# Four small tiles of a one-core diffusion step made larger, so that the tiles behind them start elsewhere in the partition

## The chip, the cores and the metric

The kernel runs on one core of one Trainium2 chip. Its time is the device time of one execution in microseconds (us); the profile's page, its trace and three timed runs of the kernel before are at hand.

## The reference, cut to what matters

One layer of a hybrid trunk: a shared input projection feeds a gated position-mixing group (A) and a latent-attention group (B); the two are gated, concatenated and projected out. 1024 latent tokens and 128 context tokens, width 1024, all in float32.

```python
def _front(x, cond, norm_g, w_ada, b_ada, w_in, w_s, b_s, g_v, q_norm_g, w_uq, kv_norm_g):
    mod = jax.nn.silu(cond) @ w_ada + b_ada
    shift, scale, gate = jnp.split(mod[:, None, :], 3, axis=-1)
    h = _rmsnorm(x, norm_g) * (1 + scale) + shift
    u, v, g_a, c_q, c_kv, k_rope, g_b = _split_in(h @ w_in)
    a_out = _chunk_mlp(u, v, w_s, b_s, g_v) * jax.nn.silu(g_a)
    ...
def _block_attention(q_nope, q_ropes, key_sets):
    ...
        s = jnp.concatenate(logits, axis=-1).astype(jnp.float32) * ATTN_SCALE
        p = jax.nn.softmax(s, axis=-1).astype(v_all.dtype)
        return jnp.einsum('bhqk,bkhv->bqhv', p, v_all)
    ...
def _back(x, gate, a_out, attn, g_b, w_o):
    y = jnp.concatenate([a_out, attn * jax.nn.silu(g_b)], axis=-1) @ w_o
    return x + gate * y
```

## The kernel before, in words

Every large product is made of three TensorE passes. An operand is split into a high part of fewer bits and the remainder (`lo_of`, line 112, makes the remainder on VectorE), and high by high, high by low and low by high are summed in PSUM. In this text a product, or pass, is one matmul of 128 rows by so many columns: its stationary operand is a 128x128 block of 512 bytes in each partition, its moving operand has 128 partitions by 256, 384, 448 or 512 columns of 4 bytes.

The stages, in order of time:
- 0 to 60 us: the inputs `x` and the conditioning weights `ada` are loaded (SP's queue), the conditioning is multiplied out, the tokens are normalised and turned, and the first products `vacc` are made (512 columns).
- 60 to 235 us: twelve blocks of 128 channels, as two-by-two block products with sums of blocks (`pair_steps`): `p` (line 928, 504 passes) and `tp` (line 949, 288 passes), all of 384 columns. Their stationary operands are the split weights `w` and the split sums `s`; the moving ones are the split tokens in `area` and their sums in `w1t`.
- 235 to 310 us: the query and key projections, `zacc` (lines 1371 to 1373, 448 columns), `qr` and `qn` (lines 158 to 160, 256 and 384 columns).
- 310 to 515 us: attention. Scores `s` (512 and 256 columns), transposes `pT` of the softmax output `e`, and `o` (lines 1633 to 1635, 256 columns; moving operands `ph` and `pl`).
- 515 to 599 us: the output projection, again as block products (`three`, lines 1970 to 1972, 512 columns): results `S` and `A`. The seven products of each of the four `PAIRS` of token tiles read as moving operand one of seven matrices. Two of these, T1 and T4, are read back from DRAM into tiles of the last pool `ep`: T1 wholly (`t1a`, `t1c`, `t1h`, `t1l`, 12 passes a pair), T4 by half (`t4`, 6 passes a pair; the trace drops the number and prints `t`), the other half lies in `vht` and `vlt` of the pool `kv`. The last products `left` (lines 1999 to 2001) have 256 columns.

Each engine's order is written out by planners (`Plan`, `merged`) with fixed costs. They don't know addresses.

Tiles lie in pools; a pool gives each tile a fixed place, rounded up to 32 bytes in the partition, one behind the other. Pools of the left side grow upwards, those of the right side downwards, each from where its neighbour ends. So a small tile sets where all that is laid out behind it starts. Of the built program, the start of a tile in its partition, as the remainder by 128 bytes:

| tiles | before | after the change |
|---|---|---|
| `area`, `w1t`, the keys and values (`kch` to `vl`, later `vht`, `vlt`), the rings `ringB`, `ringC`, `ml`, `mixA`, `ident` | 0 | 0 |
| pool `va` behind `sel`: `x`, `ada`, `w2r`, `w`, `s`, `rows` | 64 | 0 |
| the rest of `va` behind `selr` (`hf`), and of the pools `vb` and `vg` what takes part in products: `gv`, `wsT`, `adag` | 96 | 0 |
| right side below `warm_e`: `mixB`, `cqh`, `cql`, `wfh`, `wfl`, `z`, `e`, `ph`, `pl`, `os`, `t4`, `t1a`, `t1c`, `t1h`, `t1l`, `xr` | 96 | 0 |
| `wuv` (in the first pool) | 96 | 96 |

By 256 bytes, `x`, `ada` and `w2r` start at a remainder of 192 before and of 0 after.

The four tiles themselves hold a scalar or two: `early` and `warm_e` take the output of an activation that is made only to load a table, `sel` and `selr` are two columns that pick sums.

Of the kernel before, what the change touches and what calls it, by code (L numbers as in the profile page):

```python
# [9 lines left out]
F32 = mybir.dt.float32  # L10
F32R = mybir.dt.float32r
# [7 lines left out]
P = 128  # L19
# [70 lines left out]
def f32(ap):  # L90
    return ap.bitcast(F32)
# [3 lines left out]
def tile_hymba_step(ctx: ExitStack, tc: tile.TileContext, I, O):  # L95
# [3 lines left out]
    def opened(name, bufs=1, space=None, side=None):  # L99
        kw = dict(name=name, bufs=bufs, reuse_waits="tile")  # L100
        if space is not None:
            kw["space"] = space
        if side is not None:
            kw["side"] = side
        cm = tc.tile_pool(**kw)
        return cm, cm.__enter__()

    def closed(cm):
        cm.__exit__(None, None, None)
# [120 lines left out]
    c_sm, sm = opened("sm", bufs=2, side="right")  # L230
# [31 lines left out]
    c_va, va = opened("va", side="left")  # L262
# [5 lines left out]
    csp = va.tile([P, 8, 32], F32, tag="csp", name="csp")  # L268
    V.memset(csp, 0.0)
    cs = csp[:, :, 0:2].rearrange("p k c -> p c k")  # L270
    early = va.tile([P, 1], F32, tag="early", name="early")
    tc.keep_in_program_order(S.activation(early, ones[:, 0:1], AF.Silu))
    tc.keep_in_program_order(S.activation(cs, condT, AF.Silu))
    tc.keep_in_program_order(S.activation(early, ones[:, 0:1], AF.Sqrt))

    sel = va.tile([P, 2], F32, tag="sel", name="sel")
    V.tensor_reduce(sel, ident.rearrange("p (j c) -> p c j", j=4)[:, 0:2, :], axis=AX.X, op=ALU.add)

    def slot(i, name, shape, dt=F32):
# [170 lines left out]
    warm = psa.tile([P, 512], F32, tag="acc", name="warm")  # L450
# [553 lines left out]
        for c, g, m, key, room in ((i, 0, "x", "kx", "tm"), (j, 1, "d", "ke", "kd"), (j, 0, "c", "kf", "kc"), (i, 1, "a", "kh", a_room)):  # L1004
            gated(c, g, lambda m=m: keep[m], [f"{key}{n}"], (room,), lambda m=m: keep[m])

    selr = va.tile([P, 2], F32R, tag="selr", name="selr")
    V.tensor_copy(selr, sel)

    def gate_steps(j):  # L1010
# [149 lines left out]
    def rope_weights():  # L1160
        for q in range(2):
            src = rope_raw[:, q * 256 : (q + 1) * 256]
            S.activation(wrh[:, q, :], src, AF.Copy, scale=qgT[:, q : q + 1])
            V.scalar_tensor_tensor(wrl[:, q, :], src, qgT[:, q : q + 1], f32(wrh[:, q, :]), op0=ALU.mult, op1=ALU.subtract)
# [72 lines left out]
    def cq_transpose(t):  # L1237
        last = t == NT - 1
        ps = (psa if last else pst).tile([P, 512], F32, tag="acc" if last else "t", name=f"cqT{t}")
        for q in range(2):  # L1240
            T.transpose(ps[:, q * P : (q + 1) * P], zt[t][:, q * P : (q + 1) * P], ident)
        src = ps[:, 0:256].rearrange("p (q c) -> p q c", q=2)
        dh = cqh[:, :, t * P : (t + 1) * P]

        def low():
            lo_of(cql[:, :, t * P : (t + 1) * P], src, dh)
            made.add(("cq", t))

        later(0.05 if last else 0.4, lambda: S.copy(dh, src))
        later(0.42 if last else 0.85, low)  # L1250
# [6 lines left out]
    def q_nope(g, h):  # L1257
        need(*[("cq", t) for t in range(3 * g, 3 * g + 3)])
        ps = psa.tile([P, 512], F32, tag="acc", name=f"qn{g}{h}")
        gc = slice(g * GW, (g + 1) * GW)  # L1260
        passes3(ps[:, :GW], [(wfh[:, q, h, :], wfl[:, q, h, :], cqh[:, q, gc], cql[:, q, gc]) for q in range(2)])
        later(1.2, lambda: S.copy(qnh[g][:, h, :], ps[:, :GW]))
        later(1.75, lambda: lo_of(qnl[g][:, h, :], ps[:, :GW], qnh[g][:, h, :]))
# [4 lines left out]
    def q_rope(t):  # L1268
        need(("cq", t))
        ps = psa.tile([P, 512], F32, tag="acc", name=f"qr{t}")  # L1270
        sl = slice(t * P, (t + 1) * P)
        passes3(ps[:, :256], [(cqh[:, q, sl], cql[:, q, sl], wrh[:, q, :], wrl[:, q, :]) for q in range(2)])
        rot[t] = []

        def raw():
            home, tag, n = (zp, "qun", 3) if t < 7 else (aside[0], f"qun{t}", 1)
            un = home.tile([P, 4, 64], F32, tag=tag, name=f"qun{t}", bufs=n)
            rot[t] = [un]
            S.copy(un, ps[:, :256].rearrange("p (h r) -> p h r", h=4))
            if t == NS:  # L1280
                made.add(("r", t))
                return
            r1 = (zp if t < 7 else aside[0]).tile([P, 4, 64], F32, tag="qr1", name=f"qr1{t}", bufs=2 if t < 7 else 1)
            r2 = zp.tile([P, 4, 64], F32, tag="qr2", name=f"qr2{t}", bufs=2)
            rot[t] = [r1, un]
            cb = rope[:, 0, t, :].unsqueeze(1).broadcast_to([P, 4, 64])
            sb = rope[:, 1, t, :].unsqueeze(1).broadcast_to([P, 4, 64])
            V.tensor_tensor(r1, ps[:, :256].rearrange("p (h r) -> p h r", h=4), cb, op=ALU.mult)

            def turn():  # L1290
                G.tensor_tensor(r2[:, :, 0:32], un[:, :, 32:64], sb[:, :, 0:32], op=ALU.mult)
                G.tensor_tensor(r2[:, :, 32:64], un[:, :, 0:32], sb[:, :, 32:64], op=ALU.mult)
                G.tensor_tensor(r1, r1, r2, op=ALU.add)
                made.add(("r", t))

            if t == 7:
                later(2.0, turn)
            else:
                turn()

        later({7: 3.4, 8: 1.2}.get(t, 0.85), raw)
# [76 lines left out]
    mixB = pools["mixB"]  # L1378
    NOPES = {4: [(0, 0)], 5: [(0, 1), (0, 2)], 6: [(0, 3)], 7: [(1, 0), (1, 1)], 8: [(1, 2), (1, 3)]}
    if True:  # L1380
        warm_e = sm.tile([P, 1], F32, tag="warm", name="warm_e", bufs=1)
        S.activation(warm_e, ones[:, 0:1], AF.Sqrt)
        rope_weights()
        for t in range(NT):
            beside = []
            if t >= 2:
                beside.append((0.75, lambda t=t: q_rope(t - 2)))
            beside += [(1.05, lambda n=n: q_nope(*n)) for n in NOPES.get(t, [])[:1]]

            full = []  # L1390
            if t >= 1:
                full.append((0.25, lambda t=t: cq_transpose(t - 1)))
            if 1 <= t < 5:
                full.append((0.45, lambda t=t: fold(t - 1)))
            if t >= 3:
                full.append((0.45, lambda t=t: q_rope_T(t - 3)))
            if full:
                beside.append((sum(f[0] for f in full), lambda full=full: [f[1]() for f in full]))
            beside += [(1.05, lambda n=n: q_nope(*n)) for n in NOPES.get(t, [])[1:]]
            if t == NT - 1:  # L1400
                beside.append((0.45, lambda: q_rope_T(t - 2)))
                beside.append((0.75, lambda: q_rope(t - 1)))
            merged([(0.62, lambda t=t, k=k: z_chunk(t, k)) for k in range(NK)], beside)
        closed(c_w1)
        c_kv, kv = opened("kv", side="left")
        kch = kv.tile([P, 11 * P], F32R, tag="kch", name="kch")
        kcl = kv.tile([P, 11 * P], F32R, tag="kcl", name="kcl")
        krh = kv.tile([P, 11 * P], F32R, tag="krh", name="krh")
        krl = kv.tile([P, 11 * P], F32R, tag="krl", name="krl")
        vh = kv.tile([P, 11, P], F32R, tag="vh", name="vh")  # L1410
        vl = kv.tile([P, 11, P], F32R, tag="vl", name="vl")
        c_ra, ra = opened("ra", side="left")
        aside.append(ra)
        for i, (dh, dl) in enumerate(((kch, kcl), (krh, krl))):
            later(0.3, lambda dh=dh, i=i: pool_copy(dh[:, CTX0:], ctxr[:, i, :]))
            later(0.3, lambda dh=dh, dl=dl, i=i: G.tensor_tensor(dl[:, CTX0:], ctxr[:, i, :], f32(dh[:, CTX0:]), op=ALU.subtract))
        cv = [v_[:, 9:, :].rearrange("p a r -> p (a r)") for v_ in (vh, vl)]
        later(9.0, lambda: pool_copy(cv[0], ctxr[:, 2, :]))
        later(9.0, lambda: G.tensor_tensor(cv[1], ctxr[:, 2, :], f32(cv[0]), op=ALU.subtract))
        for t0, c in ((8, 1), (0, 4), (4, 4)):  # L1420
            later(4.0 if t0 == NS else 9.5, lambda t0=t0, c=c: values(t0, c))
        for cost, fn in (
            (0.45, lambda: keys(0, 4, 0)),
            (0.45, lambda: keys(0, 4, 1)),
            (0.25, lambda: cq_transpose(8)),
            (0.45, lambda: keys(4, 4, 0)),
            (0.45, lambda: keys(4, 4, 1)),
            (0.75, lambda: q_rope(8)),
            (1.05, lambda: q_nope(2, 0)),
            (1.05, lambda: q_nope(2, 1)),  # L1430
            (1.05, lambda: q_nope(2, 2)),
            (1.05, lambda: q_nope(2, 3)),
            (0.25, lambda: q_rope_T(8)),
            (0.3, last_keys),
        ):
            run((cost, fn))
        later(0.8, lambda: S.activation(warm_e, ones[:, 0:1], AF.Exp))
        catch_up(1e9)
# [396 lines left out]
    with tc.manual_schedule(engines=engines):  # L1835
# [215 lines left out]
        early = [(0.65, lambda k=k: plain(k)) for k in range(4)]  # L2051
# [145 lines left out]
    for q in range(3, len(queue)):  # L2197
        n, name, _ = queue[q]
# [279 lines left out]
```

## Time and profile before

| | us |
|---|---|
| median of 3 runs | 601.26 (601.0 to 601.28) |
| profiled execution | 600.68 |
| its span, first to last instruction | 598.9 |
| TensorE busy in it | 588.7 (98%) |
| VectorE, ScalarE, GpSimd busy | 428.7, 329.7, 213.5 |

TensorE is busy in nearly all of the span, so the time is the sum of what its instructions take one after the other. Matmuls are pipelined: the duration of one (say 0.39 us) overlaps the next, so the pace of a stream is read from the starts. The distance of two starts, times the count, is what it costs. TensorE has 2.4 columns per ns at the granted clock of 1.00; 512 columns take 213.3 ns, 448 take 186.7, 384 take 160.0, 256 take 106.7. What a pass takes beyond that is called its excess here.

### The profile page before, as it was taken

The page shows a single profiled execution, that of the slowest core. Times are in us where ns is not written, and L with a number is a line of the kernel's source. Part 1 is how long each engine was busy: PE and PEld are TensorE (multiplying, and loading weights), DVE is VectorE, ACT ScalarE, POOL GpSimd, SP SyncE. Part 2 cuts the span into 40 slices and gives each one's busy share as a digit, 9 for nine tenths or more (in the row PEclk, how much of TensorE's full clock was granted, in tenths as well). Part 3 has the DMA queues.
Part 4 walks back from the last instruction along what each step waited for, and adds up shares of the span by engine and source line. Part 5 has one row for each costly group of instructions (what it writes and reads, how often), then busy time and mean ns, then how long its engine had stood idle before and what let it go on. Part 6 is the DMA issues. An engine that isn't in the chain of part 4 may idle for free.

```text
span 598.9 us, 10175 instructions
## 1 busy us (share of the span) xinstructions
PE 588.7 (98%) x3653; PEld 527.0 (88%) x3653; DVE 428.7 (72%) x946; ACT 329.7 (55%) x771; POOL 213.5 (36%) x251
## 2 busy tenths in 40 slices
PE   8999999999999999999999999999999999999995
PEld 7578889999999999999998888888888898888884
DVE  3676888967647467476678677778788876477885
ACT  6665886434323245455567556655756462457543
POOL 2562103200000000343264345454543547269834
PEclk9999999999999999999999999999999999999998
DMA  8991002051050134100002033434242019951444
GB/s 314 366 378 74 1 4 68 1 210 71 7 207 26 45 96 138 42 1 0 2 8 71 0 106 111 156 123 142 85 144 90 1 71 307 359 178 39 140 153 161
DMA packets 31059, 67.33 MB, mean 112 GB/s; under 512 B 3344, under 2 KB 17440, under 8 KB 29984
## 3 DMA queue, kind: packets, MB, share of 16 engines
q1 hardware_dynamic: 27792, 55.93, 26.7%
q0 software_dynamic: 2352, 8.39, 4.1%
q10 hardware_dynamic: 864, 2.36, 1.2%
q8 instruction: 29, 0.48, 0.3%
q14 instruction: 22, 0.18, 0.1%
HBM read 53.45 MB, written 13.21 MB: 111 GB/s over the span
## 4 chain that ended last, share of the span: by engine, by line
PE 92%; DMA 3%; POOL 2%; DVE 1%; ACT 1%; issue 0%; SPq 0%; POOLq 0%; ACTq 0%
PE p L928 15%; PE tp L949 7%; PE pT L1609 5%; PE o L1633 3%; PE o L1635 3%; PE o L1634 3%; PE zacc L1372 2%; PE zacc L1371 2%; PE zacc L1373 2%; PE S L1970 2%; PE S L1971 2%; PE S L1972 2%; DMA ada<-in_ada_ss 2%; PE s L1526 2%; PE s L1529 2%; PE s L1528 2%
## 5 line engine op out<-in xcount | busy, mean ns | idle before, releaser
L1486 POOL TENSOR_SCALAR e<-e,rs 128x1280 f32<-128x1280 f32 x32 | 47.0, 1470 | 96.8 <-DVE rs L1485 64.7
L112 DVE TENSOR_TENSOR pl<-pT,ph 128x512 fp32r<-128x512 f32 x81 | 55.5, 686 | 32.8 <-ACT ph L1613 32.6
L1481 ACT ACTIVATE e<-s,nb,scl 128x256 f32<-128x256 f32 x64 | 56.9, 891 | 38.8 <-DVE nb L1469 26.2
L1613 ACT CAST ph<-pT 128x512 fp32r<-128x512 f32 x80 | 47.2, 590 | 40.6 <-PE pT L1609 40.3
L1219 POOL TENSOR_TENSOR kr<-z,rope 128x64 f32<-128x64 f32 x8 | 2.6, 326 | 154.6 <-ACT z L1228 154.6
L949 PE MATMUL tp<-area,w 128*128 128x384 f32 x288 | 52.5, 337 | 0.0
L1633 PE MATMUL o<-ph,vh 128*128 128x256 f32 x160 | 50.7, 317 | 0.0
L949 PEld LDWEIGHTS tp<-area,w 128*128 128x128 f32 x288 | 50.4, 188 | 0.0
L1609 PE MATMUL pT<-ident,e 128*128 128x128 f32 x320 | 47.9, 272 | 0.0
L1609 PEld LDWEIGHTS pT<-ident,e 128*128 128x128 f32 x320 | 38.9, 140 | 7.2
L1635 PE MATMUL o<-ph,vl 128*128 128x256 f32 x160 | 45.1, 282 | 0.0
L1634 PE MATMUL o<-pl,vh 128*128 128x256 f32 x160 | 44.8, 280 | 0.0
L1463 DVE TENSOR_REDUCE m<-s 128x1 f32<-128x1024 f32 x32 | 38.9, 1216 | 2.6 <-PE s L1504 2.5
L1633 PEld LDWEIGHTS o<-ph,vh 128*128 128x128 f32 x160 | 30.2, 188 | 4.7 <-ACT os L1643 2.9
L1634 PEld LDWEIGHTS o<-pl,vh 128*128 128x128 f32 x160 | 30.3, 189 | 0.4
L1635 PEld LDWEIGHTS o<-ph,vl 128*128 128x128 f32 x160 | 30.1, 188 | 0.0
L928 PE MATMUL p<-area,w 128*128 128x384 f32 x144 | 27.6, 337 | 0.0
L928 PE MATMUL p<-area,s 128*128 128x384 f32 x144 | 27.3, 337 | 0.0
L1371 PE MATMUL zacc<-w1t,area 128*128 128x448 f32 x72 | 27.0, 375 | 0.0
L928 PE MATMUL p<-w1t,s 128*128 128x384 f32 x144 | 26.6, 339 | 0.0
L1372 PE MATMUL zacc<-w1t,area 128*128 128x448 f32 x72 | 26.3, 366 | 0.0
L1373 PE MATMUL zacc<-w1t,area 128*128 128x448 f32 x72 | 26.3, 365 | 0.0
(703 smaller groups left out, 1767.8 us busy)
## 6 DMA issues: line engine op xcount, KB each, us to landing
ada<-in_ada_ss SPq DMA_DIRECT2D x16, 512.0 KB, 8.6
w2r<-in_w_t SPq DMA_DIRECT2D x12, 512.0 KB, 5.3
x<-in_x SPq DMA_DIRECT2D x9, 512.0 KB, 5.6
adag<-in_ada_g SPq DMA_DIRECT2D x4, 1024.0 KB
traw<-in_w_o SPq DMA_DIRECT2D x16, 256.0 KB, 3.0
tdram<-thi SPq DMA_DIRECT2D x32, 128.0 KB, 1.8
tdram<-traw SPq DMA_DIRECT2D x32, 128.0 KB, 1.8
wor<-in_w_o SPq DMA_DIRECT2D x8, 512.0 KB, 3.8
```

The costliest lines, as they stand in the source:

```text
L112: V.tensor_tensor(lo, src, f32(hi), op=ALU.subtract)
L928: T.matmul(banks[key], a_, b_, start=k == 0 and m == 0, stop=k == 3 and m == len(passes) - 1)
L949: T.matmul(tps[c, 2][:, :GW], w_[c][:, k, :], x_[k, 2], start=k == 0 and m == 0, stop=k == NK - 1 and m == 2)
L1371: T.matmul(ps[:, :448], a, wqh[k], start=k == 0, stop=False)
L1463: V.tensor_reduce(m[:, 0:1], lat_, axis=AX.X, op=ALU.max)
L1481: S.activation(e[:, sl], src, AF.Exp, bias=nb, scale=scl[:, t : t + 1], accum_out=su[:, i : i + 1])
L1486: G.tensor_scalar(e, e, rs, 0.0, op0=ALU.mult, op1=ALU.add)
L1609: T.transpose(ps[:, w : w + P], es[t, h][:, c * P : (c + 1) * P], ident)
L1613: later(0.5, lambda: S.copy(ph[:, :w], ps[:, :w]))
L1633: T.matmul(o, vh[:, kt, :], ph[:, sl], start=c == 0, stop=False)
L1634: T.matmul(o, vh[:, kt, :], pl[:, sl], start=False, stop=False)
L1635: T.matmul(o, vl[:, kt, :], ph[:, sl], start=False, stop=c == n - 1)
```

## The change

Four tiles are allocated larger, and the program goes on using the first one or two columns of them. No instruction is added, removed or moved: on all five queues (TensorE 2818 rows, VectorE 878, ScalarE 576, GpSimd 229, SyncE 142, with repeated ones merged) the order is the same before and after. Only addresses differ, as in the table above.

```diff
-    early = va.tile([P, 1], F32, tag="early", name="early")
+    early = va.tile([P, 16], F32, tag="early", name="early")[:, 0:1]
...
-    sel = va.tile([P, 2], F32, tag="sel", name="sel")
+    sel = va.tile([P, 16], F32, tag="sel", name="sel")[:, 0:2]
...
-    selr = va.tile([P, 2], F32R, tag="selr", name="selr")
+    selr = va.tile([P, 32], F32R, tag="selr", name="selr")[:, 0:2]
...
-        warm_e = sm.tile([P, 1], F32, tag="warm", name="warm_e", bufs=1)
+        warm_e = sm.tile([P, 32], F32, tag="warm", name="warm_e", bufs=1)[:, 0:1]
```

## Rows read from the trace of the kernel before

**Rows 1.** Page, busy time by engine, and the chain that ended last by engine
```profile
PE 588.7 (98%) x3653; PEld 527.0 (88%) x3653; DVE 428.7 (72%) x946; ACT 329.7 (55%) x771; POOL 213.5 (36%) x251
...
PE 92%; DMA 3%; POOL 2%; DVE 1%; ACT 1%; issue 0%; SPq 0%; POOLq 0%; ACTq 0%
```

**Rows 2.** Timeline of TensorE, 518 to 527 us: start, duration, instruction
```profile
518.00 0.39 PE L1970 MATMUL S<-area,area 128*128 128x512 f32 x1
...
522.76 0.40 PE L1970 MATMUL S<-t1a,ringC 128*128 128x512 f32 x1
...
525.33 0.40 PE L1972 MATMUL S<-t1h,ringC 128*128 128x512 f32 x1
525.56 0.39 PE L1970 MATMUL A<-area 128*128 128x512 f32 x1
...
526.95 0.39 PE L1970 MATMUL A<-area,area 128*128 128x512 f32 x1
```

**Rows 3.** Timeline of TensorE, 531 to 534 us
```profile
531.03 0.40 PE L1970 MATMUL A<-t,ringC 128*128 128x512 f32 x1
...
532.43 0.39 PE L1970 MATMUL A<-vht,ringC 128*128 128x512 f32 x1
...
533.81 0.40 PE L1970 MATMUL S<-t1a,area 128*128 128x512 f32 x1
```

**Rows 4.** Chain that ended last, pieces of 84 to 237 us: start, time, what
```profile
123.21 4.24 PE tp L949 x24
127.45 12.66 PE p L928 x72
140.12 4.19 PE tp L949 x24
...
165.22 4.16 PE tp L949 x24
...
201.84 25.13 PE p L928 x144
226.97 8.38 PE tp L949 x48
```

**Rows 5.** Window of line 928 alone: length, PE busy, PEld busy, clock, DMA share, GB/s
```profile
60.00:240.00 180.00, 91.35 (x504) 88.05 (x504) 1.00 0.20 73
```

**Rows 6.** Groups by line and shape: busy us, mean ns, idle before
```profile
L949 PE MATMUL tp<-area,w 128*128 128x384 f32 x288 | 52.5, 337 | 0.0
...
L112 DVE TENSOR_TENSOR pl<-pT,ph 128x512 fp32r<-128x512 f32 x81 | 55.5, 686 | 32.8 <-ACT ph L1613 32.6
...
L112 DVE TENSOR_TENSOR ringB<-raw,ringB 128x512 fp32r<-128x512 f32 x8 | 5.5, 685 | 4.6 <-ACT raw L2206 4.6
```

**Rows 7.** Timeline of TensorE, 303 to 307.3 us
```profile
303.05 0.33 PE L158 MATMUL qn<-cqh,wfh 128*128 128x384 f32 x1
...
307.21 0.27 PE L1312 MATMUL qrT<-ident,qun 128*128 128x128 f32 x1
```

**Rows 8.** Timeline of TensorE, 235 to 241 us
```profile
235.19 0.37 PE L1371 MATMUL zacc<-w1t,area 128*128 128x448 f32 x1
...
240.47 0.36 PE L1373 MATMUL zacc<-w1t,area 128*128 128x448 f32 x1
```

**Rows 9.** Timeline of TensorE in attention, 388.0 to 388.7 us
```profile
388.01 0.28 PE L1634 MATMUL o<-pl,vh 128*128 128x256 f32 x1
...
388.60 0.27 PE L1652 MATMUL at<-os,wuv 128*128 128x128 f32 x1
```

**Rows 10.** Timeline of TensorE at the end, 586 to 592 us
```profile
586.01 0.28 PE L1999 MATMUL left<-area 128*128 128x256 f32 x1
...
591.64 0.28 PE L2001 MATMUL left<-area,ml 128*128 128x256 f32 x1
```

**Rows 11.** Chain that ended last, its first DMA pieces: start, time, what
```profile
2.12 5.58 DMA x<-in_x
7.71 11.42 DMA ada<-in_ada_ss
```

## The prediction

> **What bounds the kernel now.** I read the page first: TensorE is busy 98% of the span, and it holds 92% of the chain that ended last [rows 1]. No instruction moves, so the only way to another time is that the same instructions take longer or shorter at their new addresses, and what counts is what TensorE's stream does. The one stretch in which others hold the chain for long is the start, where it runs through loads for 5.58 and 11.42 us [rows 11].
>
> Durations don't show the pace, so I went through the timelines and the pieces of the chain for stretches in which products of one shape follow each other, divided time by count, and took off the time of the columns; the rest is the excess. The table of start remainders tells which operands lay off 128 bytes. The reader is to see that the excess is not one number.
>
> - 512 columns, both operands at 0: 21 passes from 518.00 to 522.76, 226.7 ns each, excess 13.3 [rows 2].
> - 512 columns, moving operand at 96, stationary at 0: 12 passes from 522.76 to 525.56, 233.3 ns, excess 20.0 [rows 2]; again 6 passes from 531.03 to 532.43, 233.3 ns [rows 3]. The weights before and after them come from the same rings.
> - Back at 0, the next 6 passes are still slow: 525.56 to 526.95, 231.7 ns [rows 2].
> - 384 columns, moving at 0, stationary at 64: whole stretches keep one pace, but not all the same: 4.24, 4.19 and 4.16 us for 24 passes, so 176.7, 174.6 and 173.3 ns; 25.13 for 144 and 8.38 for 48 are 174.5, 12.66 for 72 is 175.8 [rows 4]. Together 58.76 us for 336 passes: 174.9 ns, excess 14.9.
> - 384 columns, both at 96: 24 passes of `qn` from 303.05 to 307.21, 173.3 ns, excess 13.3 [rows 7].
> - 256 columns, both at 0: `left`, 47 passes from 586.01 to 591.64, 119.8 ns, excess 13.1 [rows 10]. Moving at 96: `o`, 5 passes from 388.01 to 388.60, 118 ns [rows 9].
> - 448 columns, both at 0: `zacc`, 26 passes from 235.19 to 240.47, 203.1 ns, excess 16.4 [rows 8].
>
> My reading: an excess of 13.3 ns is the floor, and where the two operands lie at different remainders a stream can stay above it. `zacc` and `o` don't fit: the first is above the floor although both lie at 0, the second is not above it although they differ. So the reading is an inference, strongest for 512 columns and weak for 384.
>
> **The change part by part.**
>
> *Tiles of the pool `ep` (`warm_e`).* Each of the four pairs has 12 passes that read T1 and 6 that read T4 from there, 72 in all. Each falls from 233.3 to 226.7 ns: 72 x 6.6 = 0.48 us. The slow six after each set go with them: 6 x (231.7 - 226.7) = 0.03 us for each of 8 sets, 0.24 us. Could the cause be something else that these tiles share? They are filled from DRAM by the same queue as the parts of `area` that hold T2 and T3, and the T2 passes from 518.00 on keep the floor [rows 2]. So not the loading. I take 0.72 us; bounds 0 (another cause) and 0.72.
>
> *Stationary operands `w` and `s` (`early`, `sel`).* 504 passes of `p` [rows 5] and 288 of `tp` [rows 6] are 792. If they all ran at 173.3 as `qn` does, 792 x (174.9 - 173.3) = 1.27 us. Bounds from the nearest rows: all of them at the slowest pace seen, 176.7, is 792 x 1.8 = 1.4 us lost; all at the fastest, 1.27 won. I take 1.27, because `qn` has the same width and equal remainders, and the 512 stream at 0 finds its way back to the floor by itself, while the 384 stream stays at 174.6 or 176.7 for whole stretches.
>
> *256 columns (`ph`, `pl`, `cqh`).* `o` at 118 ns is no slower than `left` at 119.8, so nothing is to be won. If the aligned `o` settled at 119.8, its 480 passes would lose 480 x 1.8 = 0.9 us. But a run of `o` is six passes long, between other shapes, and never settles; I take 0.
>
> *Other engines.* VectorE makes the same remainder of 128x512 in 686 ns where it writes `pl` at 96 and in 685 where it writes `ringB` at 0 [rows 6]. I take 0 for VectorE, ScalarE and GpSimd; TensorE's stream covers them, and if that cover were gone a change of 1 ns in some 80 such operations would be 0.1 us.
>
> *Loads.* `x` and `ada` go to new addresses, and the chain waits 17.0 us for them [rows 11]. No load of before went to a tile that starts at a multiple of 256, so no row shows what that is worth; I take 0. The bounds are a loss of 0 and a gain of one part in 17 (a row of 4096 bytes off a multiple of 256 touches 17 such pieces in place of 16), 1.0 us.
>
> Sum: 0.72 + 1.27 = 2.0 us. With TensorE on 92% of the chain, 1.84 us arrive. The profiled execution took 600.68 us, 1.78 more than its span, and would come to 598.8; it was 0.58 under the median of the runs, from which I count: 601.26 - 1.84 = 599.4 us.
>
> Against this speaks a rule of the Trainium skill. The page "SBUF — State Buffer", section Specifications (TRN2), gives lines of 16 bytes and a price only for crossing to a new line, and 64 and 96 are multiples of 16: by that page no product would gain, and the time would stay at 601.26. The trace differs, with 233.3 against 226.7 ns for 512 columns [rows 2], so I go by the trace.
>
> **The rivals.**
>
> *Only the 512-column passes gain.* The three paces of the 384-column stream may come from the moment at which a stretch begins and not from the stationary operand's address. For it: the paces change between stretches that all have the same remainders, and `zacc` is at 16.4 with both at 0. Then 0.72 comes, and the 384 stretches draw their paces anew, anywhere between 1.27 won and 1.4 lost: about 601.26 - 0.7 = 600.6 us, from 599.4 to 601.9.
>
> *Nothing changes.* The 20.0 ns could belong to the region or the pool and not to the remainder. Against it: `qn` from the same upper region runs at the floor. 601.26 us.
>
> *Slower: equal remainders collide.* If both operands and what VectorE and ScalarE write now start in the same place of a line, reads could get into each other's way, and the 384 stream would pay the 20.0 ns that the 512 stream pays now: 792 x (180.0 - 174.9) = 4.0 us, less 0.72, 3.3 us, of which 3.0 arrive: 604.3 us. It decides, against the gain, from (1.2 + 0.7) / 792 = 2.4 ns a pass. Against it: `qn` at 96 and 96, and the 512 stream at 0 and 0, are at the floor [rows 2, 7].
>
> *The loads get faster too.* As a mechanism of this kernel: each row of 4096 bytes of `x` and `ada` now begins at a multiple of 256 and is written in 16 pieces. At 6 units of 32 bytes saved in 134, 17.0 us fall by 0.76 [rows 11], and with the products' 1.84 the time is 598.7 us. The Trainium skill has such a rule in "DMA: Bandwidth & Descriptors", section How a descriptor splits into AXI transactions: a start off 256 bytes costs the beats ahead of it. No run here shows it, and the page speaks of bytes fetched, while the sources in DRAM don't move.
>
> **How the numbers follow.** Both widths gain: 0.48, 599.4 us, from 598.6 to 600.2. Only 512: 0.28. Nothing: 0.10. Faster loads too: 0.07. Collision: 0.07. The first is the likeliest and gives the time. The range 598.5 to 601.4 leaves out the collision, a tenth of the other cases, and what the 384 stretches could lose at worst. A change of under 0.2%, 1.2 us, can hardly be told from none here. Faster than 600.06 are nearly all of the first case, a fifth of the second and the loads: 0.58. Within 0.2% are the rest of these two and the third: 0.34. Slower than 602.46: the collision and a little of the second, 0.08.
>
> **What would show each step.** In the changed profile: the T1 and T4 sets at 226.7 ns with no slow six behind them; every long `p` or `tp` piece of 24 at 4.16 us, and the 144 at 24.96; `zacc`, `o`, `left` and the `pl` remainders as before; the first pieces of the chain still 5.6 and 11.4 us. The prediction is wrong if long `p` pieces still show 4.19 or 4.24, if the T1 sets stay at 233, or if TensorE waits for an engine for which it did not wait before.

## The result, and the profile after

The kernel after takes 602.22 us (median of 22 runs, 601.57 to 603.15), the kernel before in the same runs 601.27 us (600.82 to 602.02). The ratio is 1.0015 with a 95% interval of 1.0009 to 1.0021: about 0.95 us slower, where 1.84 us of gain were predicted. The profiled execution took 601.72 us with a span of 599.9. The mean granted clock of TensorE was 0.997 in it and in the profile of the kernel before, so the clock does not make the difference.

The page of the kernel after: busy time by engine, and the chain that ended last by engine.

```profile
PE 590.8 (98%) x3653; PEld 528.8 (88%) x3653; DVE 427.9 (71%) x946; ACT 329.8 (55%) x771; POOL 212.5 (35%) x251
...
PE 94%; DVE 2%; DMA 2%; POOL 1%; SPq 1%; ACT 0%; issue 0%; POOLq 0%; ACTq 0%
```

The count of instructions is the same, TensorE is busy 2.1 us longer [rows 1], and no other engine is busy longer by more than 0.1. So the time went into the pace of the products, as the prediction said it would have to; only the sign is other. The pieces of the chain that ended last in the stretch of the 384-column products (start, time, what) say where:

```profile
122.92 4.22 PE tp L949 x24
127.14 12.67 PE p L928 x72
139.81 4.22 PE tp L949 x24
...
165.11 4.21 PE tp L949 x24
...
201.84 25.33 PE p L928 x144
227.17 8.45 PE tp L949 x48
```

Before, the pieces of 24 stood at 4.24, 4.19 and 4.16 us [rows 4]. Now all have nearly one pace, 25.33 / 144 = 175.9 ns, and it is neither the floor of 173.3 nor the worst. The change did act on these products, the same way on all of them, and the wrong way.

The timeline of TensorE (start, duration, instruction) at the first T1 set and the first T4 set of the kernel after:

```profile
524.01 0.40 PE L1970 MATMUL S<-t1a,ringC 128*128 128x512 f32 x1
...
526.58 0.39 PE L1972 MATMUL S<-t1h,ringC 128*128 128x512 f32 x1
526.80 0.39 PE L1970 MATMUL A<-area 128*128 128x512 f32 x1
...
528.18 0.39 PE L1970 MATMUL A<-area,area 128*128 128x512 f32 x1
...
532.26 0.40 PE L1970 MATMUL A<-t,ringC 128*128 128x512 f32 x1
...
533.65 0.39 PE L1970 MATMUL A<-vht,ringC 128*128 128x512 f32 x1
```

Twelve T1 passes take 2.79 us, 232.5 ns each; before they took 233.3 [rows 2]. The six T4 passes take 231.7 ns from these rounded starts. So the sets did not come down to the 226.7 ns of their neighbours; only the slow six behind a T1 set are a little shorter, 230 ns against 231.7.

And in the attention, four score products with the transposes behind them, in the kernel after:

```profile
403.66 0.40 PE L1526 MATMUL s<-kch,area 128*128 128x512 f32 x1
...
404.59 0.60 PE L1609 MATMUL pT<-ident,e 128*128 128x128 f32 x4
```

and the same four in the kernel before:

```profile
402.97 0.40 PE L1526 MATMUL s<-kch,area 128*128 128x512 f32 x1
...
403.88 0.60 PE L1609 MATMUL pT<-ident,e 128*128 128x128 f32 x4
```

They take 0.93 us where they took 0.91, although neither of their operands moved. To see what each stage lost I read five starts from the timeline of TensorE in each kernel, the first `p`, the first `zacc`, the first `s`, the first `S` and the last `left`. For the kernel after:

```profile
60.78 1.22 PE L928 MATMUL p<-area,w 128*128 128x384 f32 x6
...
235.46 0.36 PE L1371 MATMUL zacc<-w1t,area 128*128 128x448 f32 x1
...
240.83 0.37 PE L1373 MATMUL zacc<-w1t,area 128*128 128x448 f32 x1
...
307.88 0.47 PE L1500 MATMUL s<-kch,area 128*128 128x512 f32 x1
...
518.57 0.39 PE L1970 MATMUL S<-area,area 128*128 128x512 f32 x1
...
592.74 0.28 PE L2001 MATMUL left<-area,ml 128*128 128x256 f32 x1
```

and for the kernel before, where `zacc` begins at 235.19 [rows 8] and the last `left` at 591.64 [rows 10]:

```profile
61.05 1.22 PE L928 MATMUL p<-area,w 128*128 128x384 f32 x6
...
307.57 0.47 PE L1500 MATMUL s<-kch,area 128*128 128x512 f32 x1
...
517.32 0.39 PE L1970 MATMUL S<-area,area 128*128 128x512 f32 x1
```

The distances, less those of the kernel before, are the first row of the table at the end of the experiments: blocks (`p` to `zacc`) +0.54 us, projections +0.05, attention +0.94, output projection -0.16 (the table takes the starts to the ns). Stages whose tiles an edit leaves in place repeat in the later profiles within 0.03 us, but for the projections, which move by up to 0.12. What lies ahead of the first `p` differs between executions, from 60.78 to 62.15 us over the twelve profiles, so I judge an edit by its stages and by the timed runs, not by the span of one profile.

### The profile page after: what moved, and what is told of

The parts are those of the page before. It is cut to its first block, busy times and chain, and to the rows that moved or that the text cites. A ratio compares the mean times of both kernels' runs of the same rounds, so it can differ in the third digit from the quotient of the medians.

```text
span 599.9 us, 10175 instructions
## 1 busy us (share of the span) xinstructions
PE 590.8 (98%) x3653; PEld 528.8 (88%) x3653; DVE 427.9 (71%) x946; ACT 329.8 (55%) x771; POOL 212.5 (35%) x251
## 4 chain that ended last, share of the span: by engine, by line
PE 94%; DVE 2%; DMA 2%; POOL 1%; SPq 1%; ACT 0%; issue 0%; POOLq 0%; ACTq 0%
PE p L928 15%; PE tp L949 7%; PE pT L1609 6%; PE o L1633 4%; PE o L1635 3%; PE o L1634 3%; PE zacc L1371 2%; PE zacc L1373 2%; PE zacc L1372 2%; PE S L1972 2%; PE S L1970 2%; PE S L1971 2%; PE s L1527 2%; PE s L1528 2%; PE s L1526 2%; PE s L1529 2%
```

## The experiments

The theory with which I went into them: what counts is not that both operands have the same remainder by 128, but the **difference of the two starts, moving minus stationary, modulo some larger power of two**. By 256 bytes, `area`, `w1t`, the keys, values and rings start at 128. Before, `w` and `s` start at 192, the tiles of the right side at 96; the change puts both at 0, so that the pairs of `area` or `w1t` with `w` and `s`, and those of left and right (all but `os` with `wuv`), are now 128 apart. The main rival: a fixed loss that comes with equal remainders (the collision of the prediction).

**Streams by themselves.** The whole computation is left out: TensorE runs streams of 24 products with one difference each, for four widths, with the moving operand in the lower and then in the upper tile.

```python
w = big[st][:, 4096 + 128 * (k % 4) + 512 * (m == 2) :][:, :128]
c = off // 4 + 512 * (k % 4) + 2048 * (m == 1)
T.matmul(ps[:, :width], w, big[mv][:, c : c + width], start=i == 0, stop=i == COUNT - 1)
```

> Leaves the whole computation out: it only runs streams of 24 products, in the three-pass pattern of the kernel, one stream for each width (512, 384, 448, 256) and each difference of 0 to 480 bytes between the start of the moving and of the stationary operand (both bases lie 128 bytes past a multiple of 512), first with the moving operand low and the stationary one high in the partition, then the other way round at nine differences. Theory 1, the difference of the starts sets the pace: at 512 columns 226.7 ns at a difference of 0, and about 233 ns at 128 and at 224, in both placements; at 384 columns 173.3 at 0, and 176 at 384 (the change) and 173 to 177 at 448 (before). Theory 2, the place in the partition sets it: 512 columns at 226.7 for every difference with the moving operand low, and 233 for every difference with it high. Theory 3, the pace is drawn by the moment at which a stream begins: no order by difference, and the two placements disagree at the same difference.

The timeline of TensorE of this kernel groups each stream into one row; the 384-column streams at differences of 0, 32, 64, ... begin with `raq`:

```profile
103.96 4.32 PE L54 MATMUL raq<-low,high 128*128 128x384 f32 x24
108.12 4.32 PE L54 MATMUL rar<-low,high 128*128 128x384 f32 x24
...
120.68 4.39 PE L54 MATMUL rau<-low,high 128*128 128x384 f32 x24
124.91 4.40 PE L54 MATMUL rav<-low,high 128*128 128x384 f32 x24
...
129.15 4.36 PE L54 MATMUL raw<-low,high 128*128 128x384 f32 x24
133.34 4.35 PE L54 MATMUL rax<-low,high 128*128 128x384 f32 x24
```

From start to start: at 0 (`raq`) 4.16 us, 173.3 ns a pass; at 128 (`rau`) 4.23, 176.2; at 192 (`raw`) 4.19, 174.6. The granted clock was 1.00 from 20 to 400 us. From the starts of the single passes, without the first eight of a stream, ns a pass by the difference in bytes:

| difference | 0 | 32 | 64 | 96 | 128 | 160 | 192 | 224 |
|---|---|---|---|---|---|---|---|---|
| 512 columns | 226.7 | 233.3 | 228.9 | 233.3 | 233.6 | 234.3 | 233.3 | 233.2 |
| 448 columns | 202.7 | 206.7 | 200.0 | 205.3 | 204.0 | 206.7 | 202.2 | 204.5 |
| 384 columns | 173.3 | 173.3 | 173.3 | 176.8 | 176.0 | 176.8 | 174.7 | 173.4 |
| 256 columns | 120.0 | 117.8 | 117.8 | 120.2 | 118.7 | 117.3 | 113.3 | 118.2 |

The 226.7 of 512 columns at 0 is that of the stream at 256; the one at 0 is the first of all, began at a slower pace (7.60 us for its 24) and is left out. The other streams at 256 to 480 repeat the row within 0.2 ns, with two exceptions: 448 columns run at 206.7 at 256 (202.7 at 0) and at 204.5 at 288 (206.7 at 32). With the places swapped, three pairs differ by more than 1 ns: 384 at 192 runs at 173.3, 448 at 0 at 206.7, 256 at 192 at 117.8. The streams fit the stretches that the prediction measured before: T1 and T4 at a difference of 224 (233.3), `o` at 224 (118), `qn` and `left` at 0 (173.3, 119.8), `zacc` at 0 (203.1), `p` and `tp` at 192 (173.3 to 176.7: 174.7 in the table, 173.3 with the places swapped, 176.7 in the second kernel of streams below); and those after: `p` and `tp` at 128 (175.9), T1 at 128 (232.5). They don't cover the slow six behind a T1 set (231.7 at a difference of 0), since the first passes behind other products are left out of the table. `zacc`, from the two rows shown above 26 passes in 5.37 us, 206.5 ns, has gone to the other of its two paces in this first stretch, though neither of its operands moved.

**Left half and right half of the change.** First the three tiles of the left side alone:

```diff
-    early = va.tile([P, 1], F32, tag="early", name="early")
+    early = va.tile([P, 16], F32, tag="early", name="early")[:, 0:1]
...
-    sel = va.tile([P, 2], F32, tag="sel", name="sel")
+    sel = va.tile([P, 16], F32, tag="sel", name="sel")[:, 0:2]
...
-    selr = va.tile([P, 2], F32R, tag="selr", name="selr")
+    selr = va.tile([P, 32], F32R, tag="selr", name="selr")[:, 0:2]
```

> Only the three tiles of the left side are enlarged, warm_e stays small: stationary w and s start 256 bytes past a multiple of 512 as in the change, the right side as before. Theory 1: the 384-column products at 176.0 ns as in the change (0.6 us more than before), the attention and the end as before: 601.9 us. Theory 3: the 384-column stretches at paces between 173.3 and 176.7 in another mixture than in the change: 600.0 to 602.5. If the loss is in the attention alone: 601.3.

Then `warm_e` alone:

```diff
-        warm_e = sm.tile([P, 1], F32, tag="warm", name="warm_e", bufs=1)
+        warm_e = sm.tile([P, 32], F32, tag="warm", name="warm_e", bufs=1)[:, 0:1]
```

> Only warm_e is enlarged: the right side as in the change, the left side as before. Theory 1: the 384-column stretches keep the paces of before, the attention is 0.9 us slower as in the change (o and s), the end 0.2 us faster: 602.0 us. If the left side alone loses: 601.2.

Measured against 601.12 us: the left half 601.40 us, 1.0007 (0.9998 to 1.0016), the right half 602.01 us, 1.0013 (1.0004 to 1.0022). The left half can't be told from no change by its timed runs; its stages show the loss. By stages the halves add up to the change: the blocks lose 0.54 us with the left half and nothing with the right, the attention loses 0.99 with the right and nothing with the left.

**Both sides at 128.** `early` and `sel` go to another pool, which puts `w` and `s` at 128, and `warm_e` takes 64 elements, which puts the right side at 128: the products of all four stages, but for small ones of the gate and those with `wuv`, are at a difference of 0.

```diff
-    early = va.tile([P, 1], F32, tag="early", name="early")
+    early = vb.tile([P, 1], F32, tag="early", name="early")
...
-    sel = va.tile([P, 2], F32, tag="sel", name="sel")
+    sel = vb.tile([P, 2], F32, tag="sel", name="sel")
...
-        warm_e = sm.tile([P, 1], F32, tag="warm", name="warm_e", bufs=1)
+        warm_e = sm.tile([P, 64], F32, tag="warm", name="warm_e", bufs=1)[:, 0:1]
```

> early and sel go to another pool, so that w and s start 128 bytes past a multiple of 512, and warm_e is 256 bytes, so that the right side does too: every product of 256, 384 and 512 columns has both operands at the same remainder by 512. Theory 1: T1 and T4 at 226.7 ns with no slow six behind them (0.7 us less than before), the 384-column stretches at 173.3 (1.3 us less), the attention as before or 0.9 us slower as in the change: 599.2 to 600.2 us. Theory 2: T1 and T4 stay at 233, the 384-column products gain nothing sure: 601 to 602. Theory 3: the 384-column stretches in some other mixture, 600 to 602.5.

601.43 us, 1.0004 (0.9995 to 1.0012). The blocks gain 1.09 us and the output projection 0.53, as a difference of 0 should give. But the attention loses 1.09 and the projections 0.54, of which 0.43 are in `zacc`, whose operands stayed where they were. Equal starts are right for the long streams of 384 and 512 columns, and this placing is worse than that of before for the attention.

**Other places for the streams.** A second kernel of streams shifts both tiles together by 0, 32 and 96 bytes, and then runs streams of one difference behind short ones of other shapes.

```python
for base in (0, 8, 24):
    for width in (512, 384, 448, 256):
        for off in (0, 64, 128, 192, 224):
            stream(width, off, base, 24)
for width, off in ((384, 192), (448, 0), (256, 192), (512, 128), (512, 0), (384, 0)):
    for lead in ((256, 0, 6), (512, 96, 5), (256, 224, 7), (384, 160, 4), (512, 0, 9)):
        stream(lead[0], lead[1], 0, lead[2])
        ps = stream(width, off, 0, 24)
```

> Leaves the whole computation out, as m1_offsets does. Streams of 24 products; both operands are moved by 0, 32 and 96 bytes together, at differences of 0, 64, 128, 192 and 224 bytes; then six cases of width and difference are each started five times behind five other leading streams. If the difference by 256 bytes alone sets the pace, the common shift changes nothing: 512 columns 226.7, 228.9, 233.6, 233.3, 233.2 ns, 384 columns 173.3, 173.3, 176.0, 173.3 or 174.7, 173.4 at all three shifts. If being off a multiple of 128 has a price of its own, the shifts of 32 and 96 are slower. Behind different leads, 512 at 0 and 384 at 0 come back to 226.7 and 173.3 each time; 384 at 192, 448 at 0 and 256 at 192 show two paces (173.3 or 174.7, 202.7 or 206.7, 113.3 or 117.8) by what ran ahead.

The common shift changes nothing: 384 columns at 0, 64 and 128 settle at 173.3, 173.3 and 176.0 ns on each of the three bases. What ran before does matter. The timeline of TensorE, 384-column streams at 192:

```profile
276.30 4.35 PE L52 MATMUL rcj<-low,high 128*128 128x384 f32 x24
280.49 1.32 PE L52 MATMUL rck<-low,high 128*128 128x512 f32 x5
...
291.56 4.40 PE L52 MATMUL rcp<-low,high 128*128 128x384 f32 x24
295.80 2.23 PE L52 MATMUL rcq<-low,high 128*128 128x512 f32 x9
```

`rcj` runs at 4.19 us for 24, `rcp`, behind four products of 384 columns at 160, at 4.24; the same shape at the same difference had 4.16 earlier in this run. These are the three paces of [rows 4]. A difference of 0 at 384 columns stayed at 173.3 behind every lead tried.

**Difference 192 for `o`.** `early` and `sel` as above, `warm_e` of 16 elements and a filler of 48 elements in the pool `ep`, which puts T1 and T4 at 128, a difference of 0.

```diff
-        warm_e = sm.tile([P, 1], F32, tag="warm", name="warm_e", bufs=1)
+        warm_e = sm.tile([P, 16], F32, tag="warm", name="warm_e", bufs=1)[:, 0:1]
...
-    th[1, 3], tl[1, 3] = t1h, t1l
+    place("pad", 48, F32); th[1, 3], tl[1, 3] = t1h, t1l
```

> No operand of the attention starts at a multiple of 128. early and sel lie in another pool, so that w and s start at the remainder of area and w1t by 256 (difference 0); warm_e is 64 bytes, which moves the right side by 32 bytes, so that ph and pl lie 64 bytes below vh by 256 (difference 192 in place of 224); the last pool gets 192 bytes of padding, so that T1 and T4 have the difference 0. By the difference theory: the 384-column products 1.1 us less, the end 0.5 us less, o at 117.8 or less in place of 118.3 (0.2 to 2 us less), zacc 0 to 0.4 more: 597.5 to 599.7 us. If alignment to 128 is what counts for anything, the attention is no faster than before.

601.78 us, 1.0004 (0.9996 to 1.0013). The blocks gain 1.11, but the attention loses 0.56: by the starts of single passes `o` gains 0.03 us in all, so the 256-column floor of 113.3 ns doesn't come, and the scores lose 0.49. That `o` comes in sixes between other shapes may be the reason; no run tests it. The T1 and T4 sets gain, and TensorE waits 0.4 us for a load in the first T1 set, of which the next experiment shows more.

**Left side and `ep`, the attention untouched.** `early` and `sel` as above, and a filler of 56 elements in `ep`.

```diff
-    th[1, 3], tl[1, 3] = t1h, t1l
+    place("pad", 56, F32); th[1, 3], tl[1, 3] = t1h, t1l
```

> As e5_diff192, but the right side lies as before (o at the difference 224) and only the last pool is padded, by 224 bytes: differences 0 for the 384-column products of pair_steps and for T1 and T4. By the difference theory 1.1 us less there, 0.5 us less at the end, the attention as before, zacc 0 to 0.4 us more by how its stream begins: 599.4 to 600.0 us. Without it: 601.1.

600.99 us, 0.9995 (0.9986 to 1.0004), with 1.10 us gained in the blocks and 1.21 lost in the output projection, though its T1 and T4 sets come to 226.7 ns but for two pauses, the longer of them a wait for a load. The waits of TensorE there (engine and line, what it waited for, us in total, times, longest) and the timeline of GpSimd, first the waits:

```profile
PE S L1971 <- DMA t1l<-tdram: 1.4, 1, 1.4
```

```profile
505.79 1.21 POOL L115 TENSOR_SCALAR area<-wor 128x512 fp32r<-128x512 f32 x2 [3.80 <-DMA wor<-in_w_o]
510.80 0.59 POOL L1966 DMA_DIRECT2D t1a<-tdram  x1 [3.80 <-DVE area L112]
```

and GpSimd's timeline in the kernel before:

```profile
507.17 1.21 POOL L115 TENSOR_SCALAR area<-wor 128x512 fp32r<-128x512 f32 x2 [3.93 <-DMA wor<-in_w_o]
508.32 0.59 POOL L1966 DMA_DIRECT2D t1a<-tdram  x1
```

The filler moved the low end of `t1a` by 224 bytes into the place of `wor7`, a raw weight piece that VectorE still reads. So its load, which before was issued 1.15 us behind the start of the `area` pieces, is issued 5.0 us behind it; the loads behind it on GpSimd's queue come late too, `t1l`, the last that the T1 set needs, lands 12.1 us after its issue (7.7 before, by the list of issues), and TensorE waits for it. An address is also a dependence.

**The 448-column weights 64 bytes further**, to a difference of 64:

```diff
-            c = (0, 896, 1792, 3072, 3968, 4864, 6144, 7040)[k]
+            c = 16 + (0, 896, 1792, 3072, 3968, 4864, 6144, 7040)[k]
```

> Everything at the addresses of before, but the split weights of zacc are written 16 columns (64 bytes) further on in w1t: difference 64 in place of 0, so no longer at a multiple of 128. By the difference theory the 216 products of 448 columns go from about 202.7 to 200.0 ns, 0.6 us less: 600.5 us. If a start at a multiple of 128 is best: 601.1 or more.

600.78 us against 601.25, 0.9992 (0.9983 to 1.0001). The start of `zacc` in TensorE's timeline:

```profile
235.68 0.37 PE L1371 MATMUL zacc<-w1t,area 128*128 128x448 f32 x1
...
240.89 0.37 PE L1373 MATMUL zacc<-w1t,area 128*128 128x448 f32 x1
```

These 26 passes take 5.21 us, 200.4 ns, against 203.1 [rows 8]; the stage is 0.28 us shorter, half of what was expected, and no other stage moved. The interval just reaches 1.

**The left side alone, at a difference of 0**:

```diff
-    early = va.tile([P, 1], F32, tag="early", name="early")
+    early = vb.tile([P, 1], F32, tag="early", name="early")
...
-    sel = va.tile([P, 2], F32, tag="sel", name="sel")
+    sel = vb.tile([P, 2], F32, tag="sel", name="sel")
```

> Edit to the kernel before: the two smallest tiles of the left pool are taken from another pool, so that w, s and the inputs of the 384-column products start at 128 past a multiple of 512, as the area and w1t do; nothing else moves, the order on every engine is that of before. Theory (the difference of the two starts modulo 256 sets the pace): difference 0, tp and p settle at 173.3 ns; p -0.7 us, tp -0.4 us in their starts, all else as before: 600.2 us (599.9 to 600.5). Rival (any multiple of 128 is as good as another): 384-column stretches as in the changed kernel, 176.0 ns and no gain, 601.3 to 602. Second rival (the gain of the earlier kernel with both edits was taken up by a later wait whatever is moved): 601.0.

600.04 us against 601.14, 0.9983 (0.9974 to 0.9992). The chain of waits in the stretch of the blocks:

```profile
122.77 4.16 PE tp L949 x24
126.93 12.48 PE p L928 x72
139.41 4.16 PE tp L949 x24
...
200.70 24.96 PE p L928 x144
225.66 8.32 PE tp L949 x48
```

Every piece is at 173.3 ns: the 4.16 for 24 and 24.96 for 144 which the prediction named for the changed kernel. Nothing later gives the 1.1 us back.

**The left side and the 448-column weights together**, the last two edits in one kernel.

> The edit of the kernel with the left side alone, and the weights of the 448-column products 64 bytes further, together. Theory: the two add up, -1.1 and -0.3 to -0.45 us: 599.8 us (599.4 to 600.2), the 448-column stretch at 200.0 ns. Rival (the loads behind the projections bound what can be gained there): no more than the left side alone.

599.69 us against 601.14, 0.9977 (0.9967 to 0.9987): they add up.

**These, and T1 and T4 at a difference of 0 without the late load.** The filler in `ep` stays, and one like it behind the `e` tiles of the attention moves `wor7` out of the way, with all six `e` tiles.

```diff
-        e = ap_.tile([P, 1280], F32, tag="e", name=f"e{t}{h}", bufs=6)
+        e = ap_.tile([P, 1280], F32, tag="e", name=f"e{t}{h}", bufs=6); len(es) == 1 and ap_.tile([P, 56], F32, tag="pad", name="apad")
...
-    th[1, 3], tl[1, 3] = t1h, t1l
+    place("pad", 56, F32); th[1, 3], tl[1, 3] = t1h, t1l
```

> The left side, the 448-column weights, and the tiles of T1 and T4 224 bytes further down, with a filler of 224 bytes in the attention pool as well, behind its e tiles, so that t1a does not reach into the place of wor7: the order and the waits on every engine are those of before. Theory (the kernel that moved left side and T1, T4 lost what it gained because its filler let t1a's load wait for DVE's last reader of wor7): t1a is issued 1.1 us behind the start of POOL's last area piece as in before, no wait for t1l, the T1 and T4 sets at 226.7 ns, S and A together 0.6 us shorter than in before: 599.2 us (598.8 to 599.6). Rival (the loads of T1 and T4 are late by themselves as soon as the sets come earlier): PE waits for t1l again, 1 us or more, 599.8 or more. Rival (e tiles at 128 past a multiple of 512 slow the transposes and the o products, as the both-at-128 kernel lost in the attention): pT and o together 0.4 us or more above before.

599.77 us, 0.9977 (0.9968 to 0.9985): no more than without. The output projection gains 0.52 us and TensorE waits for no load, so the late load did take the gain of the earlier kernel. But the attention loses 0.63, though only the `e` tiles moved in it, the stationary operands of the transposes. The rival of the `e` tiles named this loss, but not its place: from each start to the next, the scores lose 0.50 us and `o` 0.23, though the operands of neither moved, and the transposes themselves gain 0.07.

**The same gain without touching the attention**: `t1l` and `t1c` ahead of `gate0` and `fg`, the filler last, so that `t1a` stays off `wor7`.

```diff
-    t1h, t1a = place("t1h", 512), place("t1a", 2048)
+    t1h, t1l, t1a, t1c = (place(*a) for a in (("t1h", 512), ("t1l", 512), ("t1a", 2048), ("t1c", 1024)))
     gate0, fg = place("gate0", 1024, F32), place("fg", 1024, F32)
-    t1c, t1l = place("t1c", 1024), place("t1l", 512)
+    place("pad", 56, F32)
```

> The left side and the 448-column weights as before in the kernel that joined them, and T1 and T4 at difference 0 by another way: t1l and t1c are placed ahead of gate0 and fg and the filler of 224 bytes behind them, so that t1a stays off wor7's place and the attention's tiles stay where they are in before; the order of instructions on every engine is that of before. Theory (the kernel with all three edits gained 0.52 us in S and A and gave back 0.66 in the attention because its e tiles moved): S and A 0.5 us shorter than in before, s, pT and o as in before: 599.2 us (598.9 to 599.5). Rival (the attention is slower by a state that comes with the program, whatever stands where): s and o again 0.5 us or more longer, 599.8. Second rival (t1c now lies on the place of a late e tile, its load holds up the queue and t1l comes late): PE waits for a load in the T1 set, 599.7 or more.

599.06 us (598.33 to 599.2, 7 runs) against 600.84, 0.9969 (0.9958 to 0.998): 1.8 us faster than before, and by the two ratios (0.9969 and 1.0015) 2.8 faster than the changed kernel. The T1 set in TensorE's timeline:

```profile
521.11 0.39 PE L1970 MATMUL S<-t1a,ringC 128*128 128x512 f32 x1
...
523.83 0.39 PE L1970 MATMUL A<-area 128*128 128x512 f32 x1
```

2.72 us for twelve, 226.7 ns, and the attention is as before. All 300 passes of `S` and `A` now take 68.00 us, 226.7 ns each, against 68.70 before. In the kernel ahead of this one they took 68.18, with a pause in one later T1 set; why it is gone here stays open.

All kernels by stage, us against the profile of the kernel before (its stages: 174.14, 72.37, 209.75, 74.33), the sum of the four, and the ratio of the timed runs less one, times the time before:

| kernel | blocks | projections | attention | output projection | sum | timed |
|---|---|---|---|---|---|---|
| after | +0.54 | +0.05 | +0.94 | -0.16 | +1.37 | +0.9 |
| left half | +0.54 | +0.12 | +0.03 | 0.00 | +0.69 | +0.4 |
| right half | -0.01 | -0.04 | +0.99 | -0.16 | +0.78 | +0.8 |
| both sides at 128 | -1.09 | +0.54 | +1.09 | -0.53 | +0.01 | +0.2 |
| difference 192 | -1.11 | +0.20 | +0.56 | +0.20 | -0.15 | +0.2 |
| left side and `ep` | -1.10 | +0.11 | +0.02 | +1.21 | +0.24 | -0.3 |
| 448-column weights | +0.01 | -0.28 | 0.00 | 0.00 | -0.27 | -0.5 |
| left side at 0 | -1.10 | +0.08 | -0.03 | 0.00 | -1.05 | -1.0 |
| left and 448 | -1.07 | -0.29 | -0.03 | 0.00 | -1.39 | -1.4 |
| and T1, T4, `e` moved | -1.10 | -0.30 | +0.63 | -0.52 | -1.29 | -1.4 |
| and T1, T4, reordered | -1.10 | -0.26 | -0.03 | -0.69 | -2.08 | -1.9 |

Each row of stages is from one profile. The timed ratios are uncertain by about 0.0009, 0.5 us, each way; sum and timed column differ by at most 0.54 us.

## Why the prediction was wrong, point by point

**The floor and the excess** were read rightly, and so was that addresses act on them. The experiment with the left side at 0 changes nothing but addresses and takes 1.1 us off. The rule of the Trainium skill that was weighed, "SBUF — State Buffer", Specifications (TRN2), has lines of 16 bytes and a penalty for each cross to a new one. All starts that were moved are multiples of 32, so by that rule alone none of these steps would be there.

**The failed step** is the reading that 13.3 ns "is the floor, and where the two operands lie at different remainders a stream can stay above it", with the remainder by 128. The streams show that it is the difference of the starts modulo 256. Equal remainders by 128 leave 0 or 128, and 128 is off the floor at 512 and 384 columns (233.6 and 176.0 ns in the streams). All of the rows at the floor on which I rested it have pairs of one side (`qn`, `left`, the T2 passes), whose difference is 0 by 256 as well; no row had one of 128, so the rows of before could not tell the two readings apart. The warnings were `zacc` and `o`, which I noted as not fitting and set aside, and the starts by 256, which I worked out for the loads alone.

**T1 and T4, 0.72 us.** The size was right, the premise not: at a difference of 0 the output projection gains 0.52 to 0.69 us (the 0.69 with every pass at 226.7 ns), at the 128 that the change gives it gains 0.16.

**`w` and `s`, 1.27 us.** Again the size: 1.10 us in the blocks at a difference of 0. The change gave 128 in place of 192, 175.9 ns in place of the mean of 174.9, and the blocks lost 0.54. 792 passes by 1.0 ns would be 0.8; from each start to the next, all of `p` and `tp` together lost 0.60.

**256 columns, 0 us.** Missed, and the largest loss. I expected short runs of `o` not to settle and so not to change. The bound of 0.9 us of loss that the prediction gives was the right order, for another reason: the attention lost 0.94 us. From each start to the next, `o` lost 0.46 us and the score products 0.54, and the scores' own operands did not move. Only what runs between them did, and moving only the transposes' operands slows the attention too (0.63 us).

**Other engines and loads, 0.** Right for VectorE, whose remainders `pl` take 687 ns against 686 [rows 6]:

```profile
L112 DVE TENSOR_TENSOR pl<-pT,ph 128x512 fp32r<-128x512 f32 x81 | 55.6, 687 | 33.8 <-ACT ph L1613 33.5
```

For the loads, the first pieces of the chain did not stay at 5.58 us for `x` and 11.42 for `ada` [rows 11]. In the kernel after the chain runs through one load for long (start, time, what):

```profile
4.08 9.06 DMA x<-in_x
```

The first `p` starts at 60.78 us there, where `x` begins at 0 by 256, at 61.05 in the kernel before, and at 60.78 in the one with the left side at 0, where `x` begins at 128. With a spread of 1.4 us over the profiles, no gain or loss from there is shown.

**The rivals.** That nothing changes because the pace belongs to the region or the pool is excluded for T1 and T4: they come down to 226.7 ns within the same pool. The collision named the right sign and the wrong cause: equal starts do reach the floor, and 2.4 ns a pass was not needed, since the attention did most of it and `p` and `tp` lost 0.60 / 792 = 0.8 ns a pass. That the 384 stretches draw their paces anew was half right: at 192 the pace depends on what ran before, but it is not free: at 0 it stayed at 173.3 in every run, at 128 at 176.0.

**What stays open.** Why the pace depends on the difference modulo 256, and how one product's addresses act on the next. The attention was slower at each of the four other places of the right side or the `e` tiles that were tried (differences for `o` of 0, 128, 192 and, with only the transposes moved, 224). In all four the transposes changed too: `ident` minus `e` is 32 before, and there 0, 128, 64 and 0, in the same order. No run moved `ph` and `pl` alone, so what the place of `o` costs by itself is not shown. No rule for that mix was found, and the kernel before is the best of those tried.

## What to carry to other kernels

Where TensorE alone sets the time, measure the pace of a stream from its starts, and look at moving start minus stationary start in the partition, modulo 256: here, in streams of one shape, a difference of 0 was the floor at 512 and 384 columns, 64 at 448. For short runs of several shapes in turn, as in the attention, the runs give no such rule, and only a timed run tells. Aligning every tile to 128 bytes does not give this; two sides each aligned to 128 can end 128 apart, and the kernel got slower for it. Change one pool at a time and read each stage, since moved tiles can make another stage slower or let a load wait for a reader that it did not overlap before.

## What the runs showed of the hardware that was not expected

In streams of 24, the pace of products with three operand pairs in turn takes few values, set by width and difference modulo 256 and the same on three common bases: 226.7 to 234.3 ns at 512 columns, 173.3 to 176.8 at 384, 200.0 to 206.7 at 448, 113.3 to 120.2 at 256. At 256 columns equal starts are among the slowest, 120.0, and a difference of 192 the fastest, 113.3. Some pairs have two or three paces and keep the one they fell into for a whole stretch: 384 columns at 192 ran at 173.3, 174.7 and 176.7, 448 at 0 at 202.7 and 206.7, 256 at 192 at 113.3 and 117.7, by what ran ahead of them.
